# Heads 0 and 1 beside the second hyena projection, the heads' part of the output projection beside the second half of the convolution, the output matrix gated and split ahead

## The chip, the cores and the metric

The kernel runs on one core of a Trainium2 chip, in one launch. The metric is the device time in microseconds (us) of an execution: the median of the runs shown. Engines are named as in the profile: PE (TensorE, matmuls), PEld (its weight loads), DVE (VectorE), ACT (ScalarE), POOL (GpSimd) and SP (SyncE, which here issues the DMAs). Each engine takes its own instructions in order and waits for the others by semaphores.

## The reference

One block of a hybrid network on 2048 tokens of width 1024, with 256 context tokens. A normed and modulated input goes through one wide projection. Half of the channels take a short convolution, a gate and a long convolution by FFT ("hyena"); the other half is gated linear attention (GLA) with four heads, in both directions. Both halves meet in the output projection; an MLP with squared ReLU follows.

```python
mod = jax.nn.silu(c) @ w_ada[l] + b_ada[l]
...
sh1, sc1, g1, sh2, sc2, g2 = jnp.split(mod[:, None, :], 6, axis=-1)
...
hy_l, q_l, k_l, v_l, og_l, gf_l, gb_l = jnp.split(h_lat @ w_in[l], PROJ_SPLITS, axis=-1)
...
o_l, _, _ = _gla_bidir(qh_l, kh_l, vh_l, lgf_l, lgb_l, s_f, s_b)
y_gla_l = _gla_output(o_l, og_l, gla_norm[l])
...
y_hy_l = _hyena_gate_conv(u_l, _hyena_spectrum(seq, *filt), hyena_bias[l])
...
x = x + g1 * (jnp.concatenate([y_hy_l, y_gla_l], axis=-1) @ w_out[l])
h2 = _rms_norm(x, norm_mlp[l]) * (1.0 + sc2) + sh2
x = x + g2 * _sq_relu_mlp(h2, w_mlp1[l], w_mlp2[l])
```

## The kernel before

Every f32 matmul of the projections is made of three in fp32r, a rounded format: an operand is split into a high part (`hi`, a cast on ACT) and the rest (`lo`, a subtraction on DVE) by `split`, and `mm3` (L222 to L224) adds hi x hi, lo x hi and hi x lo in PSUM. PSUM has eight buffers of 128 x 512, all from `pt`. All loads and stores are issued by SP. Intermediate results go through DRAM tensors whose names begin with `d_` (`d_u`, `d_x0`, `d_q`, `d_yt`, ...).

The stages run in this order. (1) The filter's spectrum and the context. (2) For each half of the tokens (two blocks `tb` of 512): four token-major groups (`token_major`, output `pv`), the gates (`gates`, outputs `pq`, `pk`), and the hyena projection (`hyena_in`, output `ph`), which takes 8 steps a half: four channel groups `i` by two blocks, each with three outputs of 24 matmuls, evacuated by `conv` (ACT, then two DVE instructions into tiles `cv`). Each step ends with two calls of `mod_block`, which makes one 128-column piece of the remaining modulation vector (`g1`, `sh2`, `sc2`, `g2`; 32 pieces): two loads into `mwt`, eight DVE instructions into the accumulator `mac` (L711, L713), one PE matmul that sums over partitions (L715, output `pm`), and a DVE addition (L716). `mac` and `mwt` have two buffers each. (3) The long convolution (`conv_steps`, two halves of 256 channels, each with a phase `u`, a phase `k` and a phase `y`) beside heads 0 to 2 (`attention_steps`: `states` with a scan of 62 DVE instructions, `weights`, `outputs`, `back`). (4) Head 3 beside the loading and splitting of the output matrix. (5) The output projection: per tile of 128 tokens two halves, `proj_half(t, 0)` for the hyena channels and `proj_half(t, 1)` for the heads' channels, each 24 matmuls; then the gate row `g1b` is multiplied in, `x` is added, and the tile is normed, transposed and stored as `d_h2`. Near its end the MLP's first operands are filled through one tile `raw` (one buffer). (6) The two MLP products, the second with the final norm.

Which instruction stands where on an engine is decided by `run`: it takes several generators and always advances the one that is least far by its own weight, from the tables in `W`; the recorded order is then rearranged a little within each engine by a scheduler. On the chip the order of each engine is fixed.

```python
for j in (2 * (4 * i + tb), 2 * (4 * i + tb) + 1):
    mod_block(j)
...
run((conv_steps(), W["conv"]), (attention_steps((0, 1, 2)), W["att"], W["start"]))
...
run((load_wos(), W["wo"]), (attention_steps((3,)), W["end"]))
```

Of the kernel before, what the change touches and what calls it, by code (L numbers as in the profile page):

```python
# [10 lines left out]
F32 = mybir.dt.float32  # L11
# [7 lines left out]
P = 128  # L19
# [105 lines left out]
def layout(x):  # L125
# [49 lines left out]
    for n in ("zt", "dft_u", "dft_f", "dft_i", "dft_y", "reset", "attm"):  # L175
# [6 lines left out]
         c_proj=2.7, c_gate=1.0, k_gen=1.0, k_turn=0.86, k_gap=1.51, conv=80.0, u=1.0, k=1.0, y=1.0, att=127.0,  # L182
         start=0.03, pd=0.9, scan=1.5, wts=3.4, outs=3.18, back=0.78, sq=2, wo=5.53, end=8.98, warm=14)
# [24 lines left out]
def hybrid_block(ctx: ExitStack, tc, a, out, dbg=None):  # L208
# [35 lines left out]
    d_m = dr.tile([32, P, T], F32, name="d_m")  # L244

# [36 lines left out]
    sp = sb("sp", stack=e1)  # L282
    hpa = sb("hta", stack=e1)

# [368 lines left out]

    eb1 = ctx.enter_context(ExitStack())
    hpb, hpc = sb("htb", side="right", stack=eb1), sb("htc", stack=e1)
    hts.append(ht_block(hpb))
    ap = sb("ap", stack=e1)
# [65 lines left out]
    def gates(tbs):  # L723
# [5 lines left out]
        def chain(t):  # L729
# [3 lines left out]
            for d in range(2):  # L733
# [3 lines left out]
                eb = ap.tile([P, 512], F32, tag="eb", bufs=4, name="eb")  # L737
                en = ap.tile([P, 512], F32, tag="en", bufs=4, name="en")
# [55 lines left out]
    def hyena_in(i, tbs):  # L794
        xvh, xvl = load_w(a["wi_xv"][i])
        x0h, x0l = load_w(a["wi_x0"][i])
        for tb in tbs:
            cv = []
            for h_, l_, c0, ct in ((xvh, xvl, 0, 4 + i), (xvh, xvl, P, 8 + i), (x0h, x0l, 0, i)):
                ps = pt("ph")  # L800
                wide(ps, h_, l_, c0, tb)
                cc = ap.tile([P, 512], F32, tag=("eb", "en", "ed")[len(cv)], bufs=4, name="cv")
                conv(ps, ct, cc)
                cv.append(cc)
            rows, cols = slice(i * P, (i + 1) * P), slice(tb * 512, (tb + 1) * 512)
            u, v_, x0 = cv
            gps.tensor_mul(u[:], u[:], v_[:])
            dma(d_u[rows, cols], u[:])
            gps.tensor_scalar(x0[:], x0[:], normc[:, i:i + 1], None, op0=ALU.mult)
            dma(d_x0[rows, cols], x0[:])  # L810
            for j in (2 * (4 * i + tb), 2 * (4 * i + tb) + 1):
                mod_block(j)


    ef = ctx.enter_context(ExitStack())
    heads, ucs = {}, []
    gpool = lambda h: gp if h % 2 else pre

    def load_kv(h):
        kt = pre.tile([P, 16, 2, 64], F32, tag="kt", bufs=1, name="kt")  # L820
        dma(kt[:], d_kt[h])
        vv = gpool(h).tile([P, 16, P], F32, tag="vv", bufs=1, name="vv")
        dma(vv[:], d_v[:, h * P:(h + 1) * P].rearrange("(b p) e -> p b e", p=P))
        heads[h, "kv"] = (kt, vv)

    def load_u(ct):
        uc = pre.tile([P, T], F32, tag="uc", bufs=2, name="uc")
        dma(uc[:], d_u[ct * P:(ct + 1) * P, :])
        return uc

    def new_block(tb, pool):
        hts.append(ht_block(pool))
        return norm_in(a["x"][tb * 512:(tb + 1) * 512, :], 4, flat(hts[tb][0]))

    for half in range(2):
        t0, t1 = tbs = (2 * half, 2 * half + 1)
        w = [load_w(a["wi_vg"][grp]) for grp in range(2)]
        run((token_major(0, w[0], (t0,)), 1.0))
        run((token_major(1, w[1], (t0,)), 8.0), (norm_out(xs0, *hts[t1], 0), 4.0))
        run((token_major(0, w[0], (t1,)), 1.0))  # L840
        run((token_major(1, w[1], (t1,)), 1.0))
        w = load_w(a["wi_vg"][2])
        if half == 0:
            xs0 = new_block(2, hpc)
            run((token_major(2, w, (t0,)), 1.0))
            run((token_major(2, w, (t1,)), 8.0), (norm_out(xs0, *hts[2], 0), 4.0))
        else:
            run((token_major(2, w, tbs), 1.0))
        run((token_major(3, load_w(a["wi_vg"][3]), tbs), 1.0))
        gates(tbs)  # L850
        for i in range(4):
            hyena_in(i, tbs)
            if half == 1 and i == 0:
                load_kv(0)
            if half == 1 and i >= 1 and i < 3:
                ucs.append(load_u(i - 1))
        if half == 0:
            xs0 = new_block(3, hpa)
            eb1.close()
            pre = sb("pre", side="right", stack=ef)  # L860

    dve.scalar_tensor_tensor(scl2[:], mod2[:, 16:24], 1.0, prm[:, NMLP:NMLP + 8], op0=ALU.add, op1=ALU.mult)
    probe("mod2", mod2[:])
    e1.close()


    eg = ctx.enter_context(ExitStack())
    gp = sb("gp", stack=eg)
    fp = sb("fp", side="right", stack=ef)


    def ft(tag, bufs, name):
        return fp.tile([P, 512], F32, tag=tag, bufs=bufs, name=name)

    def conv_steps():
        for hc in range(2):
            cs = slice(hc * 256, (hc + 1) * 256)
            za, st = [], {}
            for i in range(2):
                if hc:  # L880
                    ucs[i] = load_u(2 + i)
                za.append(fp.tile([P, 64, 64], F32, tag="za", bufs=2, name="za"))

            def ua1(t):
                i, r4 = divmod(t, 4)
                pp = pt("pa")
                for s in range(4):
                    tr(pp[:, s * P:(s + 1) * P], ucs[i][:, 4 * r4 + s::16], ident)
                ut = ft("zt", 3, "ut")
                nc.scalar.copy(ut[:], pp[:])  # L890
                st[t] = ut

            def ua2(t):
                i, r4 = divmod(t, 4)
                ut = st.pop(t)
                z4 = za[i][:].rearrange("p w (q r) -> p w q r", r=16)
                for s2 in range(2):
                    p2 = pt("pb")
                    for s in range(2):
                        mm(p2[:, s * 256:(s + 1) * 256], ut[:, (2 * s2 + s) * P:(2 * s2 + s + 1) * P], ua[:],  # L900
                           start=True, stop=True)
                    r = 4 * r4 + 2 * s2
                    (nc.scalar.copy if s2 else dve.tensor_copy)(
                        z4[:, :, :, r:r + 2], p2[:].rearrange("p (s q w) -> p w q s", s=2, q=4))

            def k0(t):
                kk = 2 * t
                if t % 2 == 0:
                    st["f", t // 2] = ft("dff", 2, "dff")
                    dma(st["f", t // 2][:], a["dft_f"][:, kk:kk + 4, :].rearrange("p k n -> p (k n)"))  # L910
                    st["i", t // 2] = ft("dfi", 3, "dfi")
                    dma(st["i", t // 2][:], a["dft_i"][:, kk:kk + 4, :].rearrange("p k n -> p (k n)"))
# [5 lines left out]
                if t == 0:  # L918
                    dma(kr[127:128, 0:256], d_s0[:, cs])
# [63 lines left out]
            def y2(t):  # L983
# [3 lines left out]
                if h % 2 == 0:  # L987
                    st["p4"] = pt("p4")
# [582 lines left out]
```

## Time and profile before

| | us |
|---|---|
| median of 3 runs | 2692.61 (2692.5 to 2695.48) |
| profiled execution, its own time | 2698.1 |
| span of the profiled execution | 2696.3 |

The span runs from the first instruction to the last. Matmuls are pipelined, so the mean of a matmul in the lists (390 ns for 512 columns) is not its share of time; the time from one start to the next is. Instructions are named by line, engine, operation and "output <- inputs".

| stage | us from the span's start |
|---|---|
| spectrum, context | 0 to 230 |
| first half: token-major groups, gates | 230 to 391 |
| first half: hyena projection | 391 to 522 |
| second half: token-major groups, gates | 522 to 690 |
| second half: hyena projection | 690 to 818 |
| convolution, heads 0 to 2 | 818 to 1110 |
| head 3, loading of the output matrix | 1110 to 1142 |
| output projection | 1142 to 1336 |
| first MLP product | 1336 to 1957 |
| second MLP product, final norm | 1957 to 2696 |

### The profile page before, as it was taken

How to read it: one execution, taken by the hardware profiler on the slowest of the kernel's cores; microseconds unless marked ns; L12 is line 12 of the kernel's file. 1: busy time of each engine (PE TensorE's matmuls, PEld its weight loads, DVE VectorE, ACT ScalarE, POOL GpSimd, SP SyncE). 2: the span in 40 equal slices, each digit the busy share in tenths (PEclk: the TensorE clock that was granted, in tenths of full speed). 3: DMA queues.
4: the chain of work that ended last, by engine and by line, in shares of the span. 5: the costliest groups of instructions: out<-in, count | busy, mean ns of one | idle time of the engine just before them, and what ended most of it. 6: DMA issues, size and time to landing. Idle time of an engine off the chain costs nothing.

```text
span 2696.3 us, 36126 instructions
## 1 busy us (share of the span) xinstructions
PE 2549.9 (95%) x13704; PEld 2123.2 (79%) x13704; DVE 1384.1 (51%) x2320; ACT 1045.7 (39%) x1863; POOL 605.4 (22%) x568
## 2 busy tenths in 40 slices
PE   9799999999998788899899999999989999999995
PEld 5678978898887677788788887888768888888884
DVE  5755356735567676734543336333344434443654
ACT  6464342225225455334555556555421101111112
POOL 2130231214112213133233233232100000000454
PEclk9899999999999798899999999999999999999998
DMA  5425434432547678656533334333252212221422
GB/s 194 149 78 173 130 129 141 140 113 94 177 149 196 188 214 217 195 171 205 181 108 114 106 114 139 110 114 114 78 183 78 78 48 94 78 79 47 149 98 82
DMA packets 200622, 353.53 MB, mean 131 GB/s; under 512 B 21876, under 2 KB 106744, under 8 KB 192384
## 3 DMA queue, kind: packets, MB, share of 16 engines
q1 hardware_dynamic: 200448, 351.22, 41.0%
q8 instruction: 108, 1.77, 0.3%
q14 instruction: 66, 0.54, 0.1%
HBM read 246.23 MB, written 104.93 MB: 130 GB/s over the span
## 4 chain that ended last, share of the span: by engine, by line
PE 75%; DVE 8%; DMA 7%; issue 4%; POOL 3%; ACT 3%; SPq 0%; POOLq 0%; DVEq 0%; ACTq 0%
PE ps L1340 21%; PE ps L223 7%; PE ps L222 7%; PE ps L224 7%; PE ph L222 3%; PE ph L224 3%; PE ph L223 3%; PE po L223 1%; PE po L224 1%; PE po L222 1%; POOL x L1541 1%; PE pv L222 1%; PE pv L223 1%; PE pv L224 1%; DVE ss L1078 1%
## 5 line engine op out<-in xcount | busy, mean ns | idle before, releaser
L222 PE MATMUL ps<-w2h,uh 128*128 128x512 f32 x1024 | 399.6, 390 | 11.0 <-ACT uh L227 11.0
L223 PE MATMUL ps<-w2l,uh 128*128 128x512 f32 x1024 | 399.2, 390 | 0.2 <-DVE w2l L228 0.2
L224 PE MATMUL ps<-w2h,ul 128*128 128x512 f32 x1024 | 399.1, 390 | 0.0
L1340 PE MATMUL ps<-bh,wh 128*128 128x512 f32 x896 | 352.2, 393 | 9.3 <-ACT wh L227 4.4
L1340 PE MATMUL ps<-bl,wh 128*128 128x512 f32 x896 | 351.6, 393 | 0.3 <-DVE bl L228 0.2
L1340 PE MATMUL ps<-bh,wl 128*128 128x512 f32 x896 | 350.6, 392 | 0.0
L228 DVE TENSOR_TENSOR wl<-raw,wh 128x512 fp32r<-128x512 f32 x217 | 176.7, 820 | 248.9 <-ACT wh L227 248.7
L1538 DVE TENSOR_TENSOR acc<-acc,ps 128x512 f32<-128x512 f32 x192 | 131.8, 686 | 268.2 <-PE ps L224 268.2
L222 PEld LDWEIGHTS ps<-w2h,uh 128*128 128x128 f32 x1024 | 192.8, 188 | 51.3 <-ACT uh L227 11.5
L223 PEld LDWEIGHTS ps<-w2l,uh 128*128 128x128 f32 x1024 | 192.8, 188 | 40.3 <-DVE w2l L228 0.6
L224 PEld LDWEIGHTS ps<-w2h,ul 128*128 128x128 f32 x1024 | 192.6, 188 | 40.4 <-DVE ul L228 0.2
L227 ACT CAST uh<-ur 128x512 fp32r<-128x512 f32 x128 | 70.2, 619 | 367.2 <-PE ps L223 362.4
L1340 PEld LDWEIGHTS ps<-bh,wh 128*128 128x128 f32 x896 | 169.3, 189 | 49.3 <-ACT wh L227 4.8
L227 ACT CAST wh<-raw 128x512 fp32r<-128x512 f32 x217 | 134.2, 623 | 187.3 <-PE ps L1340 152.5
L1340 PEld LDWEIGHTS ps<-bl,wh 128*128 128x128 f32 x896 | 169.7, 189 | 36.7 <-DVE bl L228 1.6
L1340 PEld LDWEIGHTS ps<-bh,wl 128*128 128x128 f32 x896 | 170.0, 190 | 35.5 <-DVE wl L228 0.2
L1547 POOL TENSOR_TENSOR acc<-acc,x 128x1024 f32<-128x1024 f32 x16 | 39.9, 2491 | 632.8 <-PE ps L224 588.4
L222 PE MATMUL ph<-hth,whi 128*128 128x512 f32 x384 | 150.9, 393 | 0.0
L224 PE MATMUL ph<-hth,wlo 128*128 128x512 f32 x384 | 149.6, 390 | 0.4 <-DVE wlo L228 0.4
L222 PE MATMUL pv<-whi,hth 128*128 128x264 f32 x512 | 146.7, 287 | 3.0 <-ACT whi L227 2.9
L223 PE MATMUL ph<-htl,whi 128*128 128x512 f32 x384 | 149.4, 389 | 0.0
L223 PE MATMUL pv<-wlo,hth 128*128 128x264 f32 x512 | 145.0, 284 | 0.3 <-DVE wlo L228 0.3
(282 smaller groups left out, 4980.1 us busy)
## 6 DMA issues: line engine op xcount, KB each, us to landing
d_m<-c SPq DMA_DIRECT2D x128, 256.0 KB, 2.3
ur<-d_m SPq DMA_DIRECT2D x32, 1024.0 KB, 5.3
raw<-in_w_dram SPq DMA_DIRECT2D x31, 1024.0 KB, 5.1
xt<-in_x_dram SPq DMA_DIRECT2D x32, 512.0 KB, 6.9
mwt<-in_wada_dram SPq DMA_DIRECT2D x64, 256.0 KB, 3.0
raw<-in_w_dram SPq DMA_DIRECT2D x32, 512.0 KB, 3.5
raw<-in_wi_vg_dram SPq DMA_DIRECT2D x20, 528.0 KB, 4.9
wada<-in_wada_dram SPq DMA_DIRECT2D x16, 512.0 KB, 7.2
```

What stands on the lines that cost most here:

```text
L222: mm(ps, lh, rh, start=first, stop=False)
L223: mm(ps, lh, rl, start=False, stop=False)
L224: mm(ps, ll, rh, start=False, stop=last)
L227: nc.scalar.copy(hi, src)
L228: dve.tensor_sub(lo, src, hi.bitcast(F32))
L1078: dve.scalar_tensor_tensor(ss[64:128, m - 1, :], ss[64:128, m, :], dc[64:128, m:m + 1], ss[64:128, m - 1, :], op0=ALU.mult, op1=ALU.add)
L1340: mm(ps[:], x_[:, sl], y_[:, j, :], start=start and i == 0, stop=stop and i == 2, skip_group_check=True)
L1538: dve.tensor_add(ac, ac, pp[:])
L1541: (dve if at == 31 and p == 3 else gps).tensor_add(x2[:, hs], x2[:, hs], ac)
L1547: gps.tensor_add(acc[:, tile, :], acc[:, tile, :], x2[:])
```

## The change

It has four parts.

The 32 modulation blocks all move into the first half's hyena steps, four a step; `hyena_in` becomes a generator over all eight steps of a half, and its tiles `cv` (like `eb` and `en` of the gates) come from a pool `cvp` of eight tiles, which later serves the convolution and the MLP as well.

`wo_steps` runs beside the token-major groups of the second half: it makes `g1b`, loads the eight blocks of the output matrix, multiplies them by `g1b` on POOL, splits them and stores both parts in `d_wo`; `load_wo` brings them back. The output projection then needs no multiplication by the gate.

The second hyena projection runs beside heads 0 and 1 (`attention_first`), the first half of the convolution beside heads 2 and 3 (`attention_second`), the second half beside `proj_heads`: the heads' part of the output projection for tiles 3 to 15, kept in `pacc`, SBUF tiles that the MLP's operands use later. The rest of the output projection is `proj_half(t, 1)` for tiles 0 to 2 and `proj_half(t, 0)` for all. The attention's tiles have fewer buffers (`qi`, `ss`, `yg` one each, `az` shared), with head 2 in other tiles, and `kr` of the convolution has four in place of five.

The MLP's first weights are split over tiles 12 to 15 in place of at tile 12, and the fill of its second operand (`fill_raw(0, 1)`) moves from tile 12 to behind tile 15.

```diff
+    d_wo = dr.tile([2, P, KD, D], F32, name="d_wo")
...
-    def hyena_in(i, tbs):
...
+    def hyena_in(tbs, mods):
+        for i in range(4):
...
+                    for ks in (range(4), range(4, KD)):
...
+                        if k < 7:
+                            yield 1.0
+                    cc = cv_tile("cv")
+                    conv(ps, ct, cc)
...
+                if mods:
+                    for j in range(4):
+                        mod_block(4 * (2 * i + tb) + j)
...
-            for j in (2 * (4 * i + tb), 2 * (4 * i + tb) + 1):
-                mod_block(j)
...
+    def load_wo(pool, tags, a_):
+        wo = [pool.tile([P, 4, D], F32R, tag=t, bufs=1, name=n) for t, n in zip(tags, ("woh", "wol"))]
+        for k in range(4):
+            for i in range(2):
+                dma(wo[i][:, k, :].bitcast(F32), d_wo[i, :, 4 * a_ + k, :])
+        return wo
...
+    def wo_steps(pool):
+
+        g1b = pool.tile([P, D], F32, name="g1b")
+        gate_rows(g1b, pool, 0, "dg")
+        yield 1.0
+        for k in range(KD):
+            raw = pool.tile([P, D], F32, tag="raw", bufs=2, name="raw")
+            dma(raw[:], a["w_out"][k * P:(k + 1) * P, :])
+            gps.tensor_mul(raw[:], raw[:], g1b[:])
+            hi = pool.tile([P, D], F32R, tag="woh", bufs=2, name="woh")
+            lo = pool.tile([P, D], F32R, tag="wol", bufs=2, name="wol")
+            split(hi[:], lo[:], raw[:])
+            dma(d_wo[0, :, k, :], hi[:].bitcast(F32))
+            dma(d_wo[1, :, k, :], lo[:].bitcast(F32))
+            yield 1.0
...
-            run((token_major(2, w, tbs), 1.0))
+            run((token_major(2, w, tbs), 8.0), (wos, 9.0))
...
-    run((conv_steps(), W["conv"]), (attention_steps((0, 1, 2)), W["att"], W["start"]))
+    run((hyena_in(tbs, False), 48.0), (attention_first(), W["att1"], W["start1"]))
...
+    run((conv_steps(0), W["conv"]), (attention_second(), W["att2"], W["start2"]))
...
+    def proj_heads():
+        for t in range(3, 16):
+            load_y(yop, t, 1)
+            for h in range(2):
+                proj_half(t, 1, woa, h, True, True)
+                (nc.scalar.copy if h else dve.tensor_copy)(pacc[t, h], ys.pop((t, "p", h))[:])
+                yield 1.0
...
+        run((conv_steps(1), W["conv"]), (proj_heads(), 26.0, W["start3"]))
...
+    woc = load_wo(bqc, ("bh2", "bl2"), 0)
+    for t in range(3):
+        load_y(yop, t, 1)
+        for h in range(2):
+            proj_half(t, 1, woa, h, True, False)
...
-                dve.tensor_mul(x1[:, h * 512:(h + 1) * 512], ys.pop((t, "p", h))[:], g1b[:, h * 512:(h + 1) * 512])
-            gps.tensor_add(x1[:], x1[:], xt[:])
+                dve.tensor_add(x1[:, hs], pp[:], pacc[t, h] if t > 2 else xt[:, hs])
+            if t > 2:
+                gps.tensor_add(x1[:], x1[:], xt[:])
...
-                wops = {m: w_split(r0, m) for m in ORDER}
-                raw1 = fill_raw(0, 1, dve)
+                wops = {m: w_split(r0, m) for m in (1, 2, 6, 5)}
+            elif t > 12:
+                m = (7, 4, 3)[t - 13]
+                wops[m] = w_split(r0, m)
+            if t == 15:
+                fill_split(1, fill_raw(0, 1, dve))
```

Three places show how the instructions stand now. The first is PE in the first half's hyena projection, between two steps. Before (`ph` is a step's output, `pm` the sum of a modulation block, the number behind a name its place in the program):

```order
L222 MATMUL ph_3871<-hth_234,whi_3793 128x512
L223 MATMUL ph_3871<-htl_235,whi_3793 128x512
L224 MATMUL ph_3871<-hth_234,wlo_3794 128x512
L715 MATMUL pm_3917<-ones_82,mac_3904 128x1
L715 MATMUL pm_3933<-ones_82,mac_3920 128x1
L222 MATMUL ph_3936<-hth_2109,whi_3793 128x512
```

The same place between two steps of the changed kernel:

```order
L223 MATMUL ph_4030<-htl_2114,whi_3807 128x512
L224 MATMUL ph_4030<-hth_2113,wlo_3808 128x512
L730 MATMUL pm_4076<-ones_83,mac_4063 128x1
L730 MATMUL pm_4092<-ones_83,mac_4079 128x1
L730 MATMUL pm_4108<-ones_83,mac_4095 128x1
L730 MATMUL pm_4124<-ones_83,mac_4111 128x1
L222 MATMUL ph_4147<-hth_238,whi_4127 128x512
```

Four sums stand in a row where two stood, and the next step's first matmul stands behind the fourth.

The second place is DVE at that border, after the sums of a step. Before:

```order
L716 TENSOR_TENSOR mod2_87<-pm_3917,prm_78 128x1
L716 TENSOR_TENSOR mod2_87<-pm_3933,prm_78 128x1
L711 TENSOR_SCALAR mac_4027<-mwt_4028,sil_84 128x128
L713 SCALAR_TENSOR_TENSOR mac_4027<-mwt_4028,sil_84,mac_4027 128x128
L789 SCALAR_TENSOR_TENSOR cv_3896<-ph_3871,prm_78,cv_3896 128x8x63
```

There `mac_4027` is the first block of the next step, whose sum `pm_4040` PE reaches 72 matmuls later. In the changed kernel, after the first two sums of a step (`pm_4251` and `pm_4267`):

```order
L731 TENSOR_TENSOR mod2_88<-pm_4251,prm_79 128x1
L731 TENSOR_TENSOR mod2_88<-pm_4267,prm_79 128x1
L726 TENSOR_SCALAR mac_4270<-mwt_4271,sil_85 128x128
L728 SCALAR_TENSOR_TENSOR mac_4270<-mwt_4271,sil_85,mac_4270 128x128
L804 SCALAR_TENSOR_TENSOR cv_4230<-ph_4205,prm_79,cv_4230 128x8x63
L728 SCALAR_TENSOR_TENSOR mac_4270<-mwt_4271,sil_85,mac_4270 128x128
L806 SCALAR_TENSOR_TENSOR cv_4230<-ph_4205,prm_79,cv_4230 128x8x63
```

`mac_4270` belongs to the third sum of the same group (`pm_4283`), which is the next thing that PE has.

The third place is SP at the start of the output projection of the changed kernel (`woh`, `wol` are the two parts of the matrix for the hyena channels, `yt_11234` the heads' channels of tile 0, `xt` the input). Three more pairs of `woh` and `wol` stand ahead of these rows:

```order
L987 DMA woh_11224<-d_wo_71 128x1024
L987 DMA wol_11225<-d_wo_71 128x1024
L977 DMA yt_11234<-d_yt_67 128x4x128
L977 DMA yt_11266<-d_yt_67 128x4x128
L1336 DMA xt_11336<-in_x_dram 128x1024
L1336 DMA xt_11378<-in_x_dram 128x1024
```

Before, the first tiles of `yt` were loaded among the blocks of the matrix, while head 3 still ran; here the loads of the matrix stand ahead of the first tile.

603 lines of the change are left out of this document (308 added, 295 removed).

## The prediction

> **What bounds the kernel now.** I read the page first, then the busy time by stage, then the chain of waits and the timeline.
>
> ```profile
> PE 2549.9 (95%) x13704; PEld 2123.2 (79%) x13704; DVE 1384.1 (51%) x2320; ACT 1045.7 (39%) x1863; POOL 605.4 (22%) x568
> ```
>
> TensorE (PE) is busy 95% of the span, so a change gains only what PE loses somewhere. The table by stage shows where (columns: stage, its length, then busy time and count of each engine, granted clock, DMA share, GB/s):
>
> ```profile
> 230.00:330.00 100.00, 99.14 (x816) 97.71 (x815) 39.69 (x83) 30.79 (x56) 19.49 (x32) 1.00 0.45 140
> ...
> 391.00:522.00 131.00, 131.00 (x595) 108.98 (x593) 86.66 (x190) 33.79 (x47) 25.52 (x23) 1.00 0.42 132
> ...
> 690.00:818.00 128.00, 127.58 (x580) 105.67 (x580) 83.83 (x188) 27.29 (x36) 23.43 (x20) 1.00 0.44 141
> 818.00:968.00 150.00, 123.19 (x1163) 108.66 (x1163) 111.49 (x225) 77.13 (x143) 35.71 (x38) 0.89 0.78 212
> 968.00:1110.00 142.00, 114.56 (x1157) 100.87 (x1154) 107.99 (x229) 74.79 (x139) 34.85 (x34) 0.90 0.69 189
> 1110.00:1142.00 32.00, 28.98 (x179) 22.11 (x178) 20.33 (x34) 16.60 (x23) 5.33 (x9) 0.85 0.81 248
> 1142.00:1336.00 194.00, 189.94 (x902) 156.18 (x901) 86.11 (x128) 80.11 (x149) 65.46 (x52) 1.00 0.58 186
> ```
>
> The first row is from the token-major projections; 391 to 522 is the first hyena projection and 690 to 818 the second, both with PE full. From 818 to 1142 the long convolution and the heads run, with PE idle for 57 us and its clock granted at 0.85 to 0.90; from 1142 to 1336 comes the output projection, full again. What the change can win lies between 818 and 1142. The chain of waits gives the length of the pieces there (start, us, what; xN counts records, two for an f32 matmul):
>
> ```profile
> 821.38 1.73 PE pb L900 x8
> ...
> 922.58 1.95 PE py L978 x8
> ...
> 949.88 0.48 PE py L978 x4
> 950.36 0.84 PE p L992 x8
> 951.20 0.44 PE pp L1134 x4
> 951.64 1.09 PE pa L1090 x64
> ...
> 1018.30 0.44 PE pz L927 x4
> 1018.73 0.87 PE pu L938 x4
> 1019.60 0.89 PE p L955 x8
> 1020.49 1.02 PE po L1114 x16
> 1021.51 1.02 PE po L1118 x16
> ...
> 1348.77 283.29 PE ps L1340 x1236
> ```
>
> The same four transposes of `py` took 0.48 us at 949.88 but about 0.97 at 922.58 (eight in 1.95): there PE was busy at half clock. At full clock half of the convolution is 8 x (0.44 + 1.73) + 16 x (0.44 + 0.87 + 0.89) + 16 x (0.48 + 0.84) = 74 us of PE (the first transposes taken as those of `pz`). A head is four groups of states (1.1 each, taken as `pa`), two of weights (1.09) and four quarters of outputs (1.02 + 1.02 + 0.44): 16.5 us. So 818 to 1142 holds 2 x 74 + 4 x 16.5 = 214 us of full-clock PE work in 324 us: 110 us are there to be won at most. A 512-column matmul costs 283.29 / 1236 = 0.229 us.
>
> **The change part by part. First: four modulation blocks per step.** `mod_block` ran twice in each of the 16 hyena steps; now it runs four times in each of the first half's 8 steps and never in the second half. Each block is eight VectorE (DVE) instructions into a `mac` tile and one PE matmul, and `mac` still has two buffers. PE takes its instructions in order, and the order rows put all four `pm` matmuls between one step's `ph` and the next. The first two blocks can be made ahead. The third needs a buffer that the first `pm` of the same group releases, so DVE makes blocks three and four while PE stands at their `pm`; queued behind are all matmuls of the next step. Today the same thing happens two blocks long, but beside the next step's matmuls, so the timeline of DVE already has the price:
>
> ```profile
> 404.79 0.38 DVE L716 TENSOR_TENSOR mod<-pm,prm 128x1 f32<-128x1 f32 x2 [3.22 <-PE pm L715]
> 405.09 0.28 DVE L711 TENSOR_SCALAR mac<-mwt,sil 128x128 f32<-128x128 f32 x1
> ...
> 405.67 0.74 DVE L789 SCALAR_TENSOR_TENSOR cv<-ph,prm,cv 128x504 f32<-128x504 f32 x1
> ...
> 407.24 2.28 DVE L713 SCALAR_TENSOR_TENSOR mac<-mwt,sil,mac 128x128 f32<-128x128 f32 x5
> 410.22 0.29 DVE L711 TENSOR_SCALAR mac<-mwt,sil 128x128 f32<-128x128 f32 x1 [0.70 <-DMA mwt<-in_wada_dram]
> ...
> 413.11 1.52 DVE L713 SCALAR_TENSOR_TENSOR mac<-mwt,sil,mac 128x128 f32<-128x128 f32 x4
> ```
>
> ```profile
> 421.57 0.38 DVE L716 TENSOR_TENSOR mod<-pm,prm 128x1 f32<-128x1 f32 x2 [2.04 <-PE pm L715]
> ...
> 428.31 0.69 DVE L228 TENSOR_TENSOR wlo<-raw,whi 128x512 fp32r<-128x512 f32 x1 [0.88 <-ACT whi L227]
> ...
> 434.38 0.73 DVE L713 SCALAR_TENSOR_TENSOR mac<-mwt,sil,mac 128x128 f32<-128x128 f32 x2
> ```
>
> From `pm` to the second block's end it is 414.63 - 404.79 = 9.84 us in an even step and 435.11 - 421.57 = 13.54 in an odd one, where the split of the next weights stands between. In the changed kernel the second block has no convolution beside it (2 x 0.74 off) and one more turn to PE and back (about 0.5, as the four `pm` with their write-back today): 8.9 and 12.6. Four of each: 86 us. The lower end is DVE alone: two blocks of 0.28 + 7 x 0.38 (1.52 for four) with the write-backs, 6 us a step or 48 in all. The upper end is the rows as they stand: 94.
>
> After such a stop PE starts slowly. Behind today's longest stop:
>
> ```profile
> 1953.42 0.39 PE L1340 MATMUL ps<-bh,wl 128*128 128x512 f32 x1
> 1964.85 0.80 PE L222 MATMUL ps<-w2h,uh 128*128 128x512 f32 x1 [11.05 <-ACT uh L227]
> ...
> 1968.01 0.63 PE L223 MATMUL ps<-w2l,uh 128*128 128x512 f32 x1
> 1968.43 0.63 PE L224 MATMUL ps<-w2h,ul 128*128 128x512 f32 x1
> ```
>
> the starts are 0.42 us apart (1968.01 to 1968.43) instead of 0.229, for eight matmuls: 8 x 0.2 = 1.6 us. Eight stops: 13 us (1 to 2 us a stop: bounds 8 and 16). This part costs 86 + 13 = **+99 us**. Nothing is won for it in the second half: that stage is PE-full today, with the blocks in it.
>
> **Second: the output matrix ahead.** In the second half's token-major groups, eight blocks are loaded, multiplied on POOL, split and stored, 1.57 MB each, 12.6 MB. These groups are 2 x 8 x 24 matmuls at 100 / 816 = 0.123 us, or 47 us, and move 140 GB/s x 47 = 6.6 MB already. Two stretches of 10 us show what the DMA can do:
>
> ```profile
> 1120.00:1130.00 10.00, 10.00 (x56) 7.93 (x56) 6.77 (x12) 6.14 (x9) 2.40 (x4) 0.69 0.94 298
> ```
>
> ```profile
> 1970.00:1980.00 10.00, 9.83 (x44) 7.79 (x43) 6.48 (x9) 3.85 (x6) 0.00 (x0) 1.00 1.00 360
> ```
>
> The first, at a share of 0.94, is while this same matrix is loaded today; the second, at 1.00, loads large pieces only. At 298 GB/s 19.2 MB take 64 us, 17 over the groups' 47. So the part costs between 0 (PSUM lets PE run ahead, and the gates behind take the rest) and +17. The Silu copies that free PSUM stand among the splits on ACT, but most of the work can slip, so I go near the lower end: **+5**.
>
> The Trainium skill speaks against this part: its page "DMA: Bandwidth & Descriptors", section "Where 436 GB/s comes from", puts the limit between HBM and SBUF at about 358 GB/s. The 360 of the second row agree with it. By that limit the bytes would still take 54 us, 7 more than the groups, and my +5 would be +7.
>
> **Third: the stages from 690 on.** A, second hyena projection with heads 0 and 1: 128 + 33 = 161 us of PE; the cover is dense, yet DVE's scans share an engine with its evacuations, so I allow 6%: 171. B, first half of the convolution with heads 2 and 3: nothing dense is beside it, and it is exactly half of what runs from 818 to 1142: 324 / 2 = 162. C, second half with 26 x 12 = 312 projection matmuls: 74 + 71.5 = 145.5, plus 5%: 153. D, the other 456 matmuls and 128 transposes: 104.5 + 14 = 118.5 of PE. Its bytes are no bound by themselves: what 1142 to 1336 moves takes 0.58 x 194 = 113 us of all DMA engines, and 4 MB of the matrix come back in place of 13 tiles of heads (3.3 MB). But two waits are new. At its start the first tile of the heads is queued on SP behind those 4 MB: at 298 GB/s 14 us in which PE has nothing. At its end the fills of the MLP's operands go one after another through the one `raw` tile, and the change puts one more of them behind the last tile. A turn of that tile is 16.3 us today (chain of waits, start to start):
>
> ```profile
> 1312.49 5.16 DMA raw<-d_h
> ...
> 1328.81 5.87 DMA raw<-d_h
> ```
>
> less the MLP's 21 matmuls for its first part of the contraction (4.8): 12 late. So D is 118.5 + 14 + 12 = 144.5, with bounds at 118.5 and today's 194. Sum 171 + 162 + 153 + 144.5 = 630, against 1336 - 690 = 646 now: **-16**. The ends are -70 (A, C and D at PE's own time, B at 150 for its second half of the waits) and +35 (D as long as now).
>
> **Sum.** 2696.3 + 99 + 5 - 16 = 2784 us of span. The profiled execution took 2698.1 outside, 1.8 more than its span, and the median of the runs is 2692.6, 5.5 under it: 2784 + 1.8 - 5.5 = 2781 (rounded up from 2780.6).
>
> **Rivals.** (1) *The stops come, the gaps fill.* A, C and D run at PE's own time and B at 150: -70 instead of -16, 2727. For it: wherever 512-column matmuls fill the stage today PE does not wait. Against it: the two waits of D are in the order of SP and in a tile with one buffer. 0.25. (2) *Memory is worse than thought.* The matrix costs its +17, D stays at 194 because four stage borders now each wait for loads into tiles that the stage before still holds: 12 + 50 more, 2843. 0.11. (3) *Faster.* The stops stay at 6 us (48 + 8 = 56), because the two `mwt` buffers are always refilled in time, and the mixed stages gain over 61 us of the 110; at 80 won it is 2692.6 + 56 + 5 - 80 = 2674. It decides at 61; B alone keeps half of the 110, so A, C and D would have to be almost without loss. For it: in C the dense matmuls keep the clock up, where `py` ran at half clock. 0.05, and 0.02 for its point of no change. (4) *Part one does not do what I say*, the blocks being ready when PE comes: 2692.6 + 5 - 16 = 2682, faster too. Only a third `mac` buffer could do that, and none is there. 0.03.
>
> **How the numbers follow.** My forecast 2781 has 0.54, with 2755 to 2815 its own range. The overall range takes in rival (1) down to 2715 and rival (2) up to 2840. Measurement tells about 0.2% (5 us) from no change: faster 0.05 + 0.03 = 0.08, same 0.02, slower 0.90.
>
> **What would show it.** Right: the first hyena projection grows from 131 to about 230 us, with PE idle before `pm`, put down to DVE's `mac`, in eight stops of 8 to 13 us, and granted clock under 1.00 there; the second half of the convolution with PE above 90%; the last stage near 145 us at 230 GB/s or more. Wrong: no idle time at `pm`, or a first half of the convolution far under 160 us, or an output projection that starts without a wait.

## The result and the profile after

The changed kernel takes 2859.43 us (median of 4 runs, 2857.05 to 2861.35) against 2694.05 us (4 runs, 2692.5 to 2697.19): a ratio of 1.0612, 95% interval 1.0594 to 1.063. The direction was forecast; the time lies 78 us above the forecast and 19 us above the range. (A slip in the section on the change: the first rows of PE before show `ph_3871` with `whi_3793`, which belongs to the next step's first output; by the kernel a step's last output takes other weights. Nothing rests on it.)

The page of the changed kernel, busy time of the engines:

```profile
PE 2580.3 (90%) x13704; PEld 2140.0 (75%) x13704; DVE 1397.6 (49%) x2333; ACT 1051.6 (37%) x1876; POOL 624.4 (22%) x571
```

PE has the same 13704 matmuls as before and a lower share. The table by stage (stage, length, busy time and count of PE, PEld, DVE, ACT, POOL, granted clock, DMA share, GB/s) says where its time went:

```profile
391.00:632.00 241.00, 158.34 (x643) 130.46 (x641) 138.34 (x343) 37.51 (x52) 28.43 (x24) 0.79 0.38 117
632.00:810.00 178.00, 165.96 (x1074) 148.55 (x1075) 85.65 (x111) 65.82 (x116) 63.88 (x60) 0.94 0.47 155
810.00:1004.00 194.00, 171.98 (x1234) 136.94 (x1233) 109.24 (x228) 54.50 (x84) 40.16 (x41) 0.95 0.52 147
1004.00:1165.00 161.00, 126.19 (x1225) 109.55 (x1224) 113.66 (x243) 81.08 (x149) 36.91 (x37) 0.89 0.72 211
1165.00:1316.00 151.00, 148.54 (x856) 130.40 (x856) 60.06 (x90) 64.86 (x121) 20.77 (x16) 0.98 0.40 118
1316.00:1474.00 158.00, 125.51 (x577) 101.54 (x578) 65.77 (x84) 62.01 (x118) 53.47 (x47) 0.90 0.69 225
1474.00:1520.00 46.00, 32.47 (x111) 23.27 (x111) 29.02 (x45) 25.32 (x48) 8.90 (x8) 0.81 0.51 166
```

The first hyena projection (first row) has PE idle for 83 us and a clock of 0.79 where it was full. The stages A to D of the prediction are the third to the sixth row: 194, 161, 151 and 158 us. The seventh is the start of the first MLP product, with PE busy 32 of 46 us. The list of what PE waited for (sum, times, longest) names the causes:

```profile
PE pm L730 <- DVE mac L728: 82.7, 16, 8.2
PE po L222 <- ACT yh L227: 30.5, 3, 18.2
PE pd L1073 <- DMA vv<-d_v: 13.7, 1, 13.7
PE ps L1407 <- ACT bh L227: 13.1, 5, 5.1
...
PE pg L714 <- DVE gs L709: 10.4, 4, 8.7
```

Sixteen stops at `pm`, two in each of the eight steps, are the ones foretold. One stop looks like this on PE's timeline:

```profile
442.69 0.56 PE L730 MATMUL pm<-ones,mac 128*128 128x1 f32 x2 [5.78 <-DVE mac L728]
447.60 0.59 PE L730 MATMUL pm<-ones,mac 128*128 128x1 f32 x2 [4.35 <-DVE mac L728]
448.05 0.77 PE L222 MATMUL ph<-hth,whi 128*128 128x512 f32 x1
448.62 0.63 PE L223 MATMUL ph<-htl,whi 128*128 128x512 f32 x1
449.05 0.63 PE L224 MATMUL ph<-hth,wlo 128*128 128x512 f32 x1
...
452.46 0.62 PE L223 MATMUL ph<-htl,whi 128*128 128x512 f32 x1
452.88 0.43 PE L224 MATMUL ph<-hth,wlo 128*128 128x512 f32 x1
```

Two blocks keep PE 10 us, and then eleven matmuls start 0.43 us apart, not 0.229. Over the stage the starts of `ph` beyond 0.229 us add up to 15.3 us (before: 0.7), and the time from the last `ph` ahead of the sums to the first behind them to 96.6 us (before: 4.7).

To compare runs I take stages from the first starts of the tiles, as the timeline has them: (a) first half, first `pv` to first `ph`; (b) to the second half's first `pv`; (c) to its first `ph`; (d) to the convolution's first `pb`; (e) to its last `py`; (f) to the first MLP product's first `ps`; (g) to the second's.

| run | total | a | b | c | d | e | f | g |
|---|---|---|---|---|---|---|---|---|
| before | 2694 | 161.4 | 134.2 | 160.2 | 136.4 | 278.4 | 224.0 | 643.5 |
| after | 2859 | 159.8 | 241.0 | 175.9 | 211.3 | 293.4 | 161.3 | 655.2 |
| e1 | 2813 | 161.4 | 193.6 | 176.0 | 209.6 | 291.5 | 161.8 | 656.7 |
| e2 | 2809 | 159.1 | 191.2 | 175.9 | 211.0 | 291.6 | 160.8 | 656.3 |
| e3 | 2846 | 158.2 | 240.3 | 176.3 | 210.3 | 294.0 | 152.1 | 652.7 |
| e4 | 2851 | 161.4 | 241.2 | 176.1 | 211.0 | 291.2 | 167.5 | 640.8 |
| e5 | 2836 | 159.8 | 241.6 | 175.5 | 190.7 | 289.8 | 161.0 | 654.8 |
| e6 | 2862 | 159.8 | 240.5 | 178.8 | 210.3 | 294.0 | 162.0 | 655.4 |
| e7 | 2765 | 176.8 | 134.6 | 177.2 | 209.2 | 291.9 | 158.8 | 653.3 |
| e8 | 2734 | 174.6 | 134.6 | 182.6 | 191.1 | 290.0 | 157.8 | 641.1 |
| e9 | 2852 | 158.2 | 239.9 | 168.5 | 213.4 | 291.6 | 161.8 | 656.3 |
| e10 | 2765 | 163.4 | 134.6 | 186.7 | 209.7 | 291.8 | 161.1 | 657.5 |
| e11 | 2835 | 161.4 | 241.3 | 176.0 | 190.0 | 290.2 | 159.5 | 652.7 |
| e12 | 2738 | 166.0 | 134.6 | 195.6 | 187.0 | 291.2 | 158.3 | 642.0 |
| e13 | 2796 | 159.3 | 183.0 | 175.2 | 209.7 | 291.1 | 161.4 | 654.3 |
| e14 | 2781 | 165.1 | 153.3 | 178.5 | 209.4 | 292.5 | 160.4 | 656.5 |
| e15 | 2764 | 164.9 | 139.9 | 180.5 | 209.7 | 291.3 | 161.2 | 655.0 |
| e16 | 2721 | 161.7 | 140.2 | 176.8 | 186.7 | 290.1 | 159.1 | 643.0 |

All but e16 are single runs beside the kernel before on the same chip; the four runs of the changed kernel spread over 4 us, so less than that says nothing. Columns that an edit does not touch agree within about 3 us, except (c) where blocks were moved out of the first hyena steps (180.5 in e15). Column (f) before still holds head 3 and the loading of the matrix.

### The profile page after: what moved, and what is told of

Same layout as the page of the kernel before. It is cut to its first block, busy times and chain, and to the rows that moved or that the text cites. A ratio compares the mean times of both kernels' runs of the same rounds, so it can differ in the third digit from the quotient of the medians.

```text
span 2859.6 us, 36181 instructions
## 1 busy us (share of the span) xinstructions
PE 2580.3 (90%) x13704; PEld 2140.0 (75%) x13704; DVE 1397.6 (49%) x2333; ACT 1051.6 (37%) x1876; POOL 624.4 (22%) x571
## 4 chain that ended last, share of the span: by engine, by line
PE 52%; DVE 6%; DMA 4%; POOL 3%; issue 2%; ACT 1%; SPq 0%; POOLq 0%; DVEq 0%; ACTq 0%
PE ps L1407 20%; PE ps L222 7%; PE ps L223 7%; PE ps L224 7%; PE po L222 1%; PE po L224 1%; PE po L223 1%; POOL x L1608 1%; DVE ss L1088 1%; PE p L962 1%; POOL x L1346 1%; DMA raw<-d_h 1%; DVE bl L228 1%; PE pb L870 1%; DMA d_x<-x 1%
## 5 line engine op out<-in xcount | busy, mean ns | idle before, releaser
L222 PEld LDWEIGHTS ps<-w2h,uh 128*128 128x128 f32 x1024 | 192.6, 188 | 51.5 <-ACT uh L227 11.4
L222 PE MATMUL ph<-hth,whi 128*128 128x512 f32 x384 | 161.1, 420 | 1.9 <-ACT whi L227 1.9
L224 PE MATMUL ph<-hth,wlo 128*128 128x512 f32 x384 | 156.7, 408 | 6.5 <-DVE wlo L228 6.5
L223 PE MATMUL ph<-htl,whi 128*128 128x512 f32 x384 | 157.0, 409 | 0.0
```

What stands on the lines that cost most here:

```text
L222: mm(ps, lh, rh, start=first, stop=False)
L223: mm(ps, lh, rl, start=False, stop=False)
L224: mm(ps, ll, rh, start=False, stop=last)
```

## The experiments

### The first hyena projection: e1, e2, e7, e13, e14, e15

e1 spreads the blocks over the step:

```diff
                     cv.append(cc)
+                    if mods:
+                        mod_block(4 * (2 * i + tb) + len(cv) - 1)
...
-                    for j in range(4):
-                        mod_block(4 * (2 * i + tb) + j)
+                    mod_block(4 * (2 * i + tb) + 3)
```

> The 32 blocks stay in the first half's hyena steps and mac keeps two buffers; only the place changes: one block behind each of a step's three outputs and the fourth at the step's end, so that at most two sums stand in a row. Theory (the stops come from four sums in a row with two buffers): DVE's 138 us of that stage fit beside PE's 131, the stage falls from 241 us to 140 to 165, the total to 2760 to 2785. Rival (DVE's or the loads' mere amount is the bound, twice the blocks and 17 MB of weights in that stage): the stage stays above 200, the total above 2815.

e2 changes one number:

```diff
-        ac = ap.tile([P, P], F32, tag="mac", bufs=2, name="mac")
+        ac = ap.tile([P, P], F32, tag="mac", bufs=4, name="mac")
```

> The four sums stay in a row, mac gets four buffers in place of two (mwt keeps two). Theory (the third and fourth block can't be made ahead for want of a buffer): DVE makes three to four blocks ahead while PE runs the step's 72 matmuls, the stops fall to 0 to 4 us a step, the stage from 241 us to 145 to 175, the total to 2760 to 2795. Rival (it is the loads into the two mwt buffers, which are refilled one after another, that pace DVE): stops of 6 us or more a step stay, the stage above 190, the total above 2805.

Measured: 2813.23 and 2809.41 us, stage (b) 193.6 and 191.2. e1 lies between both expectations. e2 is within its rival's by its times, though its stops, 36.5 us or 4.6 a step, are under the rival's 6. What PE waited for in e1 from 391 to 600 us, and in e2 the same with two rows of what DVE waited for:

```profile
PE pm L730 <- DVE mac L728: 37.8, 13, 5.7
```

```profile
PE pm L730 <- DVE mac L728: 36.5, 11, 6.6
...
DVE mac L726 <- DMA mwt<-in_wada_dram: 15.3, 14, 3.1
...
DVE mac L728 <- DMA mwt<-in_wada_dram: 12.9, 7, 3.8
```

Each edit takes away a little over half of the stops, and what is left is alike, though the sums stand elsewhere. In e2 DVE itself waits 28 us for the loads into `mwt`. Two blocks in place of four take everything away; e7 puts the other 16 beside the first half's token-major groups:

```diff
+                if tbs[0] < 2 and i % 2:
+                    mod_block(next(early))
                 yield 2.7
...
-                    for j in range(4):
-                        mod_block(4 * (2 * i + tb) + j)
+                    for j in range(2):
+                        mod_block(16 + 2 * (2 * i + tb) + j)
```

> Two blocks a step in the first half's hyena projection, as in the kernel before, and the other 16 beside the first half's token-major groups, one behind every second tile of 24 matmuls; mac and mwt keep two buffers. Theory (the stops come from the count of 32 blocks in a stage of 131 us, which fills DVE with its waits, and from four sums in a row): the hyena stage falls from 241 to 131 to 140 us, the token-major groups and gates of the first half grow from 161 us by 0 to 10, the total 2745 to 2770. Rival (a sum directly behind a tile stops PE for its block wherever it is put): the token-major groups grow by 25 us or more, the total above 2780.

Measured: 2764.6 us; (b) 134.6, as before the change. But (a) grew from about 160 to 176.8 us, more than expected and less than the rival's 25. PE's timeline of e7 shows the largest piece of it, a stop not at `pm` but at the transposes of the gates' input, whose copies `gs` stand on DVE behind the blocks:

```profile
331.55 0.40 PE L718 MATMUL pg<-prm,gs 128*32 128x128 f32 x1 [5.36 <-DVE gs L711]
```

Three runs then asked what paces stage (b). e13 is e1 and e2 together. e14 keeps eight blocks in groups 0 and 1 of the first half and puts 24 on DVE, one behind each output. e15 has the same eight, 16 on DVE, and eight on POOL, begun at the step's start and summed at its end:

```diff
+    def mod_pool(j):
+        ac = ap.tile([P, P], F32, tag="macg", bufs=1, name="mac")
+        for k in range(8):
+            wt = ap.tile([P, P], F32, tag="mwtg", bufs=3, name="mwt")
+            dma(wt[:], a["wada2"][j][:, k, :])
...
+                gps.tensor_scalar(wt[:], wt[:], sc, None, op0=ALU.mult)
+                gps.tensor_add(ac[:], ac[:], wt[:])
```

> e1 and e2 together: the blocks spread over the step, and four mac buffers. Theory (e1 and e2 both ended near 190 us because DVE's own queue, 136 us of work and about 50 of its waits for loads and splits, paces the stage once 32 blocks are in it): first hyena stage 180 to 192 us, no better than each alone, the total 2800 to 2815. Rival (each removes a different half of PE's stops): 140 to 160 us, the total 2765 to 2785.

> Eight blocks beside groups 0 and 1 of the first half (free in e10), 24 in the hyena steps, one behind each output. Theory (DVE's queue paces the stage): DVE has 113 us of work and its waits for loads and splits, 145 to 165 us for the stage, the total 2770 to 2790. Rival (what stops PE is a sum ahead of its block, which one block per output never is): 134 to 140 us, the total 2750 to 2762.

> Eight blocks beside groups 0 and 1 of the first half, 16 in the hyena steps on DVE (two a step, as in the kernel before), and eight there on POOL (one a step, issued a step ahead of its sum), so three sums in a row at a step's end. Theory (DVE's queue paces the stage, not the number of sums in a row nor the loads, 12.6 MB as in e14): 134 to 142 us, the total 2752 to 2764. Rival (the loads through small buffers or three sums in a row are what counts): 150 us or more, the total above 2772.

Measured: (b) 183.0, 153.3 and 139.9 us, all within the theories; totals 2795.5 (5 us better than the theory), 2780.66 (within it) and 2764.18 (0.2 us above it). PE's wait at `pm` in this stage of the three:

```profile
PE pm L730 <- DVE mac L728: 31.1, 11, 5.9
```

```profile
PE pm L734 <- DVE mac L732: 3.2, 1, 3.2
```

```profile
PE pm L734 <- DVE mac L732: 0.4, 1, 0.4
```

The stage goes with the number of blocks on DVE, 32, 24 or 16 (183, 153, 140), though the loads of e14 and e15 have the same bytes and e15 has three sums in a row. So of the 107 us that (b) gained, some 58 were the order (four sums in a row with two buffers: 241.0 to 183.0), and 49 the amount: with 32 blocks DVE is busy 132 us in e13 and waits 21 more for `mwt` and 10 for the casts of the weights, which is more than the 134 us that the stage took before. Whether the amount costs by DVE's own work or by the refilling of the two `mwt` buffers is not shown: fewer blocks on DVE are also fewer loads through `mwt` (the blocks on POOL have three buffers of their own), and no run gives `mwt` more. DVE's wait for `mwt` is 20.6 us in e13, 12.3 in e14 and 14.2 in e15, where PE stops 0.4 us at `pm`.

### The output matrix ahead: e6, e9, e10

e6 spreads `wo_steps` over groups 2 and 3, e9 over groups 0 to 2. e10 places the modulation blocks in three parts: eight beside groups 0 and 1 of the first half, 16 in the hyena steps, eight beside groups 0 and 1 of the second half. e6:

```diff
-            run((token_major(2, w, tbs), 8.0), (wos, 9.0))
+            run((groups(w, tbs), 8.0), (wos, 1.7))
```

(`groups` is groups 2 and 3 one behind the other.) e9, with the same `*part(2)` beside group 0 of the other block and group 1:

```diff
+        part = lambda n: ((islice(wos, n), n / 10.8),) if half else ()
-        run((token_major(0, w[0], (t0,)), 1.0))
+        run((token_major(0, w[0], (t0,)), 1.0), *part(2))
...
-            run((token_major(2, w, tbs), 8.0), (wos, 9.0))
+            run((token_major(2, w, tbs), 8.0), (wos, 3 / 2.7))
```

> The eight blocks of the output matrix are spread evenly over the second half's token-major groups 2 and 3 in place of the first third of group 2. Theory (the 10 us lost there, and the wait of 8.9 us at pg, come from the blocks' splits standing in a bunch on DVE and ACT): the stage from 632 to 810 us falls from 178 to 166 to 172 us, the total to 2847 to 2854. Rival (it is the amount, 12.6 MB through the DMA queues, that costs): the stage stays at 175 or more, the total above 2856.

> The output matrix's blocks start beside the first token-major group of the second half in place of group 2: two steps beside each of groups 0, 0 and 1, three beside group 2. Theory (its eight blocks go through two buffers, load, POOL, ACT, DVE, store, in about 7 us each whatever their place, 55 us in all; where they end in group 3, DVE's copies gs stand behind them): from the second half's first pv to its first ph it takes 160 to 166 us in place of 175.9 (before: 160.2), the total is 2843 to 2850. Rival (the amount costs, wherever it is): 173 us or more, the total above 2855.

> Eight blocks beside groups 0 and 1 of the first half, 16 in the first hyena projection (two a step), eight beside groups 0 and 1 of the second half; none where norm's or the gates' work fills DVE. Theory (16 blocks cost 16 us beside the first token-major groups in e7 only because DVE was late for the copies in group 3): first pv to first ph of the first half 159 to 164 us (e7: 176.8, before: 161.4), hyena stage 134 to 136, second half's token-major stage 175 to 180, the total 2745 to 2756. Rival (each block outside the hyena steps costs PE about 1 us): first half 167 or more, second 183 or more, the total above 2760.

Measured: e6 2861.89 us with (c) at 178.8 (its rival), e9 2851.72 with 168.5 (between theory and rival), e10 2764.7 with (a) at 163.4 (its theory) and (c) at 186.7 (its rival, as the total). PE's wait at `pg` in the second half's token-major stage, in e6, e9 and e10:

```profile
PE pg L714 <- DVE gs L709: 12.9, 2, 10.1
```

```profile
PE pg L714 <- DVE gs L709: 0.3, 1, 0.3
```

```profile
PE pg L718 <- DVE gs L711: 9.9, 3, 8.5
```

DVE's timeline of the changed kernel shows what `gs` stands behind:

```profile
712.15 4.31 DVE L228 TENSOR_TENSOR wol<-raw,woh 128x1024 fp32r<-128x1024 f32 x2 [11.16 <-ACT woh L227]
...
727.59 4.16 DVE L228 TENSOR_TENSOR wol<-raw,woh 128x1024 fp32r<-128x1024 f32 x2 [9.23 <-ACT woh L227]
731.66 0.18 DVE L709 COPY gs<-pv 128x32 f32<-128x32 f32 x1
```

Two blocks of the matrix take 15 us through their chain (load, POOL, ACT, DVE, store, two buffers), and while DVE stands at a `wol`, the 0.18 us copy that PE needs stands behind it. Spreading the matrix over the place where the copy is (e6) changes nothing; beginning it earlier (e9) removes the stop and half of the 16 us. The other 8 stay open; in e9 the same work has DMA at 248 GB/s and small stops at `wlo` and `htl`. e10 leaves the matrix beside group 2, and the stop at `pg` with it (9.9 us, 10.1 in the changed kernel); its eight blocks ahead make (c) 10.8 us longer, with new stops of 5.9 us at `pm`.

### The second hyena projection with heads 0 and 1: e5, e11

e5; e11 has `yield 12.0` and `att1=102.0`:

```diff
         load_q(0)
+        yield 10.0
         yield from states(0)
```

> In the second hyena projection the loads for head 0 are issued as in the changed kernel, but the first instructions of its states follow some six pieces of 12 hyena matmuls later (a pause of 10 in the heads' own count). Theory (that stage takes 194 us in place of 171 because PE stands 13.7 us at the first states for the load of vv, and runs at half clock behind it): the wait at vv falls to 0 to 3 us, the stage to 172 to 182 us, the total to 2838 to 2850. Rival (the loss is spread over the whole stage, in splits and scans on DVE, and what is saved at the start comes back at the end, where heads run without hyena matmuls): the stage stays within 5 us of 194, the total above 2853.

> As e5, with a pause of 12, and the heads' count runs at 102 in place of 81, so that heads 0 and 1 end with the hyena matmuls and not 15 to 30 us behind them. Theory (in e5 30 us of heads stood alone at the end): from the stage's first ph to the convolution's first pb it takes 170 to 182 us (after: 211.3, e5: 190.7; PE's own work about 164), the total is 2814 to 2828. Rival (DVE's scans set the pace of a head, so that a faster count only makes PE wait inside the stage): 187 us or more, the total above 2831.

Measured: 2835.83 and 2834.91 us; (d) 190.7 and 190.0 in place of 211.3. The same 40 us from 807 on, of the changed kernel and of e5:

```profile
807.00:847.00 40.00, 25.85 (x148) 20.63 (x149) 14.05 (x33) 12.61 (x23) 1.28 (x1) 0.83 0.81 220
```

```profile
807.00:847.00 40.00, 40.00 (x219) 32.31 (x218) 20.36 (x39) 16.92 (x29) 4.15 (x3) 1.00 0.87 237
```

What stands behind it in the changed kernel, a row of SP and one of PE:

```profile
815.84 0.38 SPq L1040 DMA_DIRECT2D vv<-d_v  x1
...
827.26 2.08 PE L1073 MATMUL pd<-vv,kt 64*128 64x128 f32 x16 [13.68 <-DMA vv<-d_v]
```

PE stands at the states of head 0 for a load that SP issued 2.3 us after PE came there (827.26 - 13.68 = 813.58), and the hyena matmuls behind it in PE's queue wait too; in e5, 71 more matmuls ran in the same 40 us. The pause alone gives 20.6 us in (d): the wait of 13.7, the slow start behind it, and the stops of `ph` for the weights' splits and casts, 8.4 us in the changed kernel and 0.3 in e5. The wait itself was 2.3 us until the issue and 11.4 of loading, with 2 MB of other loads issued just ahead. Here the theory of e5 held, and the total came out 2 us better than it said. e11 fell to its rival: the heads end with the matmuls now (their tail is 12 us, not 30), but the matmuls ahead of it took longer by the same amount (178 us from the first `ph` to the last, 160 in e5; waits of PE for `wlo` of 3.4 us at the longest, behind DVE).

### The output projection and the MLP's first operands: e3, e4

e3, and below it e4:

```diff
+    for t in range(2):
+        load_y(yop, t, 1)
     woc = load_wo(bqc, ("bh2", "bl2"), 0)
```

```diff
             elif t == 12:
+                fill_split(1, fill_raw(0, 1, dve))
+            elif t == 13:
                 r0 = w_raw(0)
...
-            if t == 15:
-                fill_split(1, fill_raw(0, 1, dve))
```

> Only the start of the output projection changes: the loads of the heads' channels of tiles 0 and 1 stand ahead of the 4 MB of the matrix on SP. Theory (the 18.2 us at the start are those loads queued behind the matrix): PE's wait there falls to 2 to 6 us, the stage from 158 to 140 to 148, the total to 2842 to 2850. Rival (the matrix itself is late, so PE stops at tile 2 or at the first use of the matrix instead): a new wait of 8 us or more at woh, the total above 2852.

> The fill of the MLP's second operand goes back from behind tile 15 to tile 12, and the load of the MLP's first weights moves from tile 12 to tile 13, so that one turn of the single raw tile stands behind the last tile in place of two. Theory (the first MLP product lost 26 us because one more turn of raw stands behind the last tile): the first MLP product falls from 655 us to 633 to 642, the output projection stays within 5 us of 158, the total 2837 to 2848. Rival (the waits come from the slow start of PE and from the loads of the stage, not from the turn): the first MLP product stays above 648 and the total above 2852.

Measured: e3 2845.83 us. PE's first matmul of the stage, in the changed kernel and in e3:

```profile
1332.82 0.80 PE L222 MATMUL po<-woh,yh 128*128 128x512 f32 x1 [18.20 <-ACT yh L227]
```

```profile
1318.79 0.80 PE L222 MATMUL po<-woh,yh 128*128 128x512 f32 x1 [8.72 <-ACT yh L227]
```

The wait halves and is not 2 to 6 us: on SP these loads still stand behind the convolution's last store and are issued at 1315.15. The total is within the theory's range. e4: 2850.84 us, 3 above its theory. The first MLP product falls from 655.2 to 640.8, as expected, and the stage ahead of it grows by 6, 1 more than expected. The chain of waits of the changed kernel shows the three fills one after another, PE with little to do between them:

```profile
1476.34 6.53 DMA raw<-d_h
...
1490.37 5.41 DMA raw<-d_h
...
1502.66 4.63 DMA raw<-d_h
```

and the first 46 us of the product in e4, against 32.47 us of PE and a clock of 0.81:

```profile
1478.00:1524.00 46.00, 41.54 (x170) 32.36 (x170) 32.17 (x45) 27.22 (x52) 17.14 (x11) 0.94 0.47 155
```

### All together: e8, e12, e16

e8 holds the edits of e7, e6, e5, e3 and e4; e12 those of e10, e9, e11, e3 and e4; e16 those of e15, e9, e11, e3 and e4.

> All five edits at once: 16 blocks beside the first token-major groups, the matrix spread, head 0 later, the heads' first tiles loaded ahead of the matrix, the fill of the MLP's second operand at tile 12. Theory (the losses lie in different stages and add up): 2859 less about 100, 8, 15, 13.6 (as measured) and 8.6 (as measured), so 2700 to 2730. Rival (the stages hand their losses on): above 2740. Only below 2690 would it beat the kernel before.

> The edits of e9, e10, e11, e3 and e4 together. Theory (losses in different stages add up): 2859 less 106, 12, 35, 13.6 and 8.6, so 2675 to 2700, about the kernel before or a little faster. Rival (the stages pass losses on, as in e8, which came out at 2734): above 2710.

> e15 with the edits of e9, e11, e3 and e4. Theory (stages add up, by what each was measured at): against the kernel before 2 us more in the first token-major groups, 0 to 6 more in the first hyena stage, 8 more in the second token-major stage, 2 less from the second hyena stage to the MLP, 1.5 less in the MLP: 2698 to 2712, a ratio of 1.001 to 1.007. Rival (what was moved collides, as in e12): 2720 or more, above 1.01.

Measured: 2734.27, 2738.26 and 2720.81 us; e16, the only one with more than one run, at 1.0111 times the kernel before (1.0092 to 1.0129; before it took 2692.44 in that comparison). None beats it, and no theory held: e8 lies between its theory and its rival, e12 and e16 are the rival's. What was put into one stage collides: (c) is 195.6 in e12, where eight blocks stand beside the matrix, against 168.5 and 186.7 for each alone; PE stops 17.5 us at `pm` there, 5.9 in e10. In e16 it is 176.8, 8 more than in e9, though there only the blocks of another stage were moved (with these alone, in e15, it is 5 above the changed kernel); why, is open. Where edits touch stages of their own, the columns repeat: (b) 140.2 after 139.9, (d) 186.7 after 190.0, (g) 643.0 after 640.8.

The last run shows what the third part of the change is worth. From the second hyena projection to the first MLP product (d, e, f) it is 638.8 us before, 666.0 changed and 635.9 in e16: with the heads, the tiles and the fill put right it wins 3 us, of the 16 that were forecast.

## Why the prediction was wrong

**The sum.** Forecast: 99 + 5 - 16 = 88 us. The two profiled spans differ by 163.3 (2859.6 - 2696.3). Columns: (b) +106.8, (c) +15.7, (d to f) +27.2, (g) +11.7, the rest +1.9.

**First term, right in kind, 8 us short.** The prediction said PE would stop before `pm` for DVE's third and fourth block, 86 us with 13 at half clock behind. Measured: 92 around the sums (96.6 less 4.7) and 15. What was wrong is the ground given for it: missing `mac` buffers explain about half (e2: 49.8 of the 106.8 us). e2 and e13 show that with four buffers, and even with the blocks spread, the stage stays at 183 to 191 us. I had counted DVE's 48 us of blocks, and not that 138 us of DVE with its waits do not go into a stage of 131.

**Second term, mis-sized: +5, measured 15.7.** "Most of the work can slip" was true of the splits and not of what stands behind them on DVE (e6, e9).

**Third term, the step that failed: -16, measured +38.9 with the MLP.** Three places:

- A, "the cover is dense, ... so I allow 6%: 171". It took 194, or some 188 if both are counted from the same matmul: the 690 us from which the prediction counts its 128 lie 7.6 us behind the first `ph` (682.45), the 810 us of the changed kernel only 2.1. Dense matmuls behind a waiting instruction are no cover, since PE takes its queue in order; the first states of head 0 were ahead of their load (e5: -20.6 us for a pause). In e5 30 us of heads still stand behind the last `ph`; what (d) could lose of them is open, since e11 shortened the tail and not the stage.
- D at its start, "14 us in which PE has nothing". The wait was there, with 18.2, and e3 halves it. But the stage's own work was taken at PE's 118.5 with two waits. From its first `po` on the changed kernel needs 141.1 us, and e16, which has neither wait at full size, 148.4. The list of waits of e16 has 14.8 us at the transposes of the normed rows (`ps` there), behind DVE's `x`; in the changed kernel they are 7.0, and what else the stage loses is open:

```profile
PE ps L1397 <- DVE x L1381: 14.8, 8, 6.2
```

- The border to the MLP, "12 late" within D. The turn of `raw` was late, but inside the MLP, which I had left at its old length: e4 takes 14.4 us from it for 6.2 in the stage ahead.

B (162, measured 161) and C (153, measured 151) were right. In C, 512-column matmuls stand between the convolution's small ones and PE is busy 148.54 of 151 us; in B, where nothing dense is, the pace of the convolution and the heads is what it was before.

**Half clock.** The 13 us allowed came out at 15. Behind the stop at 447.60 eleven starts took 4.8 us, and behind the stop of 18.2 us at 1332.82 nine took 4.0 us; at 0.2 us a start that is about 2 us for each step's stops beyond their length. The Trainium skill, page "TensorE: Matmul & The Clock Gate", section "What's actually happening", has the clock full again after about 3.4 us of activity. The trace has 0.6 and 1.4 us more. Being busy is not all that counts: from 926 to 938 us of the kernel before, among the convolution's small matmuls, PE is busy all 12 us and the granted clock is 0.50.

**The range.** It reached up to 2840 by "memory is worse than thought". That rival was right that stage borders wait for loads (13.7 us at the heads' start, 18.2 at D's), and its +17 for the matrix is near the measured 15.7 by luck, as half of that was a queue on DVE. But D fell from 194 to 158 where it kept it at 194, and both loads were issued behind 2 and 4 MB of others on SP, with PE's ready matmuls behind the first of them.

## What to carry to other kernels

Dense work covers a wait only if it stands ahead of the waiting instruction in the same engine's queue: when two streams are merged by weights, put a load several microseconds of the other stream ahead of its first use, and look at the borders of stages first. Before moving small jobs into a full stage, add up the helper engine's busy time there with the waits it already has, not only the jobs: here 32 blocks on DVE did not fit beside 131 us of matmuls, while 24 cost 19 us and 16 none. Losses that were measured alone add up only where the edits have stages of their own, and (c) of e16 shows that even this is not certain.

## What was not expected of the hardware

While PE stood at the states of head 0, the DMA engines moved 387 GB/s over 5 us (share 1.01), more than in the stretches that the prediction went by:

```profile
818.00:823.00 5.00, 0.00 (x0) 0.00 (x0) 0.00 (x0) 0.00 (x0) 0.00 (x0) 0.52 1.01 387
```

The kernel before had even more for longer, near its start:

```profile
10.00:20.00 10.00, 9.47 (x30) 3.23 (x28) 7.25 (x15) 8.77 (x16) 0.75 (x2) 1.00 1.03 411
```

Both are above the limit of about 358 GB/s between HBM and SBUF of the Trainium skill's page "DMA: Bandwidth & Descriptors" (section "Where 436 GB/s comes from"), against which the prediction weighed the second term. The prediction's row of 360 only seemed to agree with it; the measurement decides, and 358 was no ceiling here. What is known of the second term's miss is a queue on DVE (half of it, by e9); (c) has 155 GB/s on the whole, and no run shows the bytes as the cause of the rest.
